# A feed-forward with held activations, a part-Strassen gate and up, and a token-major closing norm

## The chip, the core and the metric

One core of a Trainium2 chip runs the whole kernel. The metric is device microseconds of that core; the kernel before was run three times, 1559.81 to 1561.2 us, with a median of 1560.31 us.

## The reference

The function is one decoder layer over 256 tokens and a model width of 2048, in float32: a mixer (causal pooling beside a gated delta rule), an attention into 256 memory tokens, a gated feed-forward, and a last RMS norm. Only the end of it changes:

```python
def conv_glu_ffn(h, w_gate, w_up, conv_w, conv_b, w_down):
    gate = causal_dwconv(h @ w_gate, conv_w, conv_b)      # three taps over tokens, per channel
    return (jax.nn.silu(gate) * (h @ w_up)) @ w_down
...
    x = x + conv_glu_ffn(rms_norm(x, ffn_norm_g[l]), w_gate[l], w_up[l], ffn_conv_w[l], ffn_conv_b[l], w_down[l])
return rms_norm(x, final_norm_g)
```

`w_gate` and `w_up` are 2048 x 5632, `w_down` is 5632 x 2048.

## The kernel before

Every float32 operand is split into two float32r parts: `split` (L96) writes the rounded part with a cast on ACT (L97) and the remainder with a subtraction on DVE (L98). A product needs three passes: high by high, high by low, low by high.

All stages but one hold the weights. `gemm` (L144) makes 128 output channels by 256 tokens; for each of 16 k tiles a 128x128 tile of the high weights is loaded into the array and streams 512 columns (the high and the low part of the activations side by side, L139), then the low weights stream the 256 columns of the high part (L140). The two halves of the PSUM row are added afterwards (`evac`, L152). Weights come 1 MB at a time over SP's queue into three `raw` buffers, and four `whi` and four `wlo` buffers hold the split parts. The one exception is the memory's values (L690 to L692): there the activations are held, 128 tokens at a time, and 512 weight columns are streamed, three passes for each k tile and token half.

The feed-forward runs 44 times over gate tile, convolution and silu, up tile (L825 to L842). The token scale of the norm, `r3b`, is multiplied in by POOL (L831, L838), the convolution is one ACT and two DVE instructions, POOL multiplies gate by up (L841), and the result is split and kept in SBUF. Then 16 output tiles of w_down each add 44 k tiles (L854 to L858). The residual stream `xres` is channel-major, so the sum of squares of the last norm crosses partitions: a matmul with ones, a reciprocal root, a second matmul that spreads it, and 16 multiplications with nine output transfers (L861 to L875).

The order on each engine is fixed when the program is built: a scheduler takes instructions by program order as their inputs and buffers come free. Each engine then works through its list in order. Small work beside the products is put into lanes (`job`, L60) and advanced a step at a time after a matmul (`pump`, L71). Three 32 KB `big` buffers per partition hold the stages' large operands in turn.

Of the kernel before, what the change touches and what calls it, by code (L numbers as in the profile page):

```python
# [13 lines left out]
ALU = mybir.AluOpType  # L14
# [27 lines left out]
def hybrid_trunk(ctx, tc, a, out):  # L42
# [4 lines left out]
    psg = ctx.enter_context(tc.tile_pool(name="psg", bufs=3, space=bass.MemoryType.PSUM))  # L47
    psd = ctx.enter_context(tc.tile_pool(name="psd", bufs=4, space=bass.MemoryType.PSUM))
    pss = ctx.enter_context(tc.tile_pool(name="pss", bufs=1, space=bass.MemoryType.PSUM))
# [115 lines left out]
    def rfinish(sums, r, rb, name):  # L165
# [9 lines left out]
        pb = pss.tile([P, 512], F32, name=name + "pb", tag="s")  # L175
# [7 lines left out]
    def rnorm(sqs, name, bcast=True):  # L183
        r, rb = rtiles(name, bcast)

        def run():
            yield
            ps = pss.tile([P, 512], F32, name=name + "ps", tag="s")
# [5 lines left out]
    with tc.tile_pool(name="dn", bufs=1, reuse_waits="tile") as dn:  # L194
# [1 line left out]
        nc.sync.dma_start(prm, a["prm"])  # L196
        hT = big("hT", [P, KT, 2, T], F32R)
        xraw = [per.tile([P, 8, T], F32, name="xraw", tag="raw", bufs=3) for _ in range(2)]
        w0 = per.tile([P, KT, P], F32, name="w0", tag="raw", bufs=3)
# [31 lines left out]
        for c in range(4):  # L231
# [153 lines left out]
        # inverses of the 16 x 16 diagonal blocks, one block to a partition; then doubled on the tensor engine  # L385
# [320 lines left out]
    def residual(ps, f, g, ht, sqa, sql, name):  # L706
        dve.tensor_tensor(xres[:, f, :], ps[:, :T], xres[:, f, :], ALU.add)
        dve.tensor_tensor(xres[:, f, :], ps[:, T:], xres[:, f, :], ALU.add)
        if ht is not None:
            split_scaled(ht[:, f, 0, :], ht[:, f, 1, :], xres[:, f, :], pv(g, f))  # L710
        if f == 15 and sql is not None:
            act.activation(sql, xres[:, f, :], AF.Square)
            return
# [12 lines left out]
    for f in range(16):  # L726
        ps = gemm([unit(a["w_mix"][f], "wm")], lambda k: yT[:, k], [KT], "mix")
        residual(ps, f, "xa_g", h2T, sq2[0], None, "mix")
# [4 lines left out]
    oT = big("oT", [P, KT, 2, T], F32R)  # L733
    with tc.tile_pool(name="xa", bufs=1, reuse_waits="tile") as xa:
# [63 lines left out]
        h3T = big("h3T", [P, KT, 2, T], F32R)  # L798
# [9 lines left out]
        for f in range(3):  # L808
            u, ps = head[f]
            gemm_part(ps, lambda k: u(k + 12), osrc, 12, 4, KT)  # L810
            residual(ps, f, "ffn_g", h3T, sq3[0], None, "xo")
    for f in range(3, 16):
        ps = gemm([unit(a["w_xo"][f], "wo")], osrc, [KT], "xo")
        residual(ps, f, "ffn_g", h3T, sq3[0], None, "xo")
    r3, r3b, r3run = rnorm(sq3, "r3")
    job("r", r3run)

# [129 lines left out]
```

## Time and profile before

| what | value |
|---|---|
| median of three runs | 1560.31 us |
| span of the profiled execution | 1558.2 us |
| PE busy / DVE / ACT / POOL | 98% / 64% / 51% / 21% of the span |
| gate and up | 797.3 to 1296.0 us |
| down | 1296.0 to 1545.3 us |
| closing norm and output | 1545.3 to 1558.2 us |
| DMA over the span | 177 GB/s read, issued from SP alone |

The profiled execution's own time is its span, from the first to the last instruction; it lies 2.1 us under the median of the runs. Matmuls are pipelined: one has a duration of 0.40 us in the trace while the next starts 0.23 us after it, so their cost is read from start to start and not from the busy column.

### The profile page before, as it was taken

What the parts mean: (1) busy time and instruction counts of PE and PEld (TensorE: products, weight loads), DVE (VectorE), ACT (ScalarE), POOL (GpSimd) and SP (SyncE); (2) the same over time, 40 slices, a digit from 0 to 9 for tenths busy, and PEclk for the clock granted to TensorE, in tenths of its full rate; (3) what the DMA queues carried; (4) which work ended last, traced back from release to release, by engine and by line L of the source; (5) the groups of instructions that cost most, each with busy time, mean ns of one, the idle gap of its engine ahead of it and who ended that gap; (6) DMA issues with size and microseconds to landing.
All of it is one profiled execution on the core that took longest, in us unless ns stands there. A gap on an engine that the chain in (4) does not pass through costs nothing.

```text
span 1558.2 us, 22142 instructions
## 1 busy us (share of the span) xinstructions
PE 1521.3 (98%) x8714; PEld 1317.2 (85%) x8714; DVE 1002.8 (64%) x1401; ACT 798.2 (51%) x1271; POOL 330.8 (21%) x385
## 2 busy tenths in 40 slices
PE   5999999999999999999999999999999999999997
PEld 3788889888888888888888888888888888888885
DVE  7978887676544776666766666666666665545453
ACT  4555656554444554655555555555555554444442
POOL 4342532441000110000122222222222220000010
PEclk9999999999999999999999999999999999999999
DMA  5445443456555555344555555555555555555552
GB/s 202 169 164 186 148 169 122 152 186 237 191 192 193 189 183 187 136 153 154 184 186 189 181 187 183 183 188 188 190 189 189 186 183 179 185 187 188 184 192 86
DMA packets 45496, 277.31 MB, mean 178 GB/s; under 512 B 8912, under 2 KB 9552, under 8 KB 14288
## 3 DMA queue, kind: packets, MB, share of 16 engines
q1 hardware_dynamic: 45392, 275.90, 50.2%
q8 instruction: 68, 1.11, 0.3%
q14 instruction: 36, 0.29, 0.1%
HBM read 272.60 MB, written 3.28 MB: 177 GB/s over the span
## 4 chain that ended last, share of the span: by engine, by line
PE 87%; DVE 7%; issue 2%; ACT 1%; POOL 1%; DMA 1%; SPq 0%; POOLq 0%; DVEq 0%; ACTq 0%
PE up L139 10%; PE gate L139 10%; PE down L139 10%; PE up L140 5%; PE gate L140 5%; PE down L140 5%; PE mix L139 4%; PE xo L139 4%; PE xq L139 4%; PE kk L139 4%; DVE wil L98 2%; PE pvs L690 2%; PE pvs L692 2%; PE pvs L691 2%; PE xo L140 2%
## 5 line engine op out<-in xcount | busy, mean ns | idle before, releaser
L139 PE MATMUL up<-h3T,wuh 128*128 128x512 f32 x660 | 235.1, 399 | 0.0
L139 PE MATMUL gate<-h3T,wgh 128*128 128x512 f32 x660 | 235.1, 399 | 0.0
L98 DVE TENSOR_TENSOR wdl<-wd,wdh 128x1024 fp32r<-128x1024 f32 x96 | 109.4, 1140 | 124.7 <-ACT wdh L97 124.6
L140 PE MATMUL up<-h3T,wul 128*128 128x256 f32 x660 | 185.4, 281 | 0.0
L140 PE MATMUL gate<-h3T,wgl 128*128 128x256 f32 x660 | 185.3, 281 | 0.0
L97 ACT CAST wdh<-wd 128x1024 fp32r<-128x1024 f32 x96 | 93.9, 978 | 135.2 <-PE down L139 127.1
L139 PEld LDWEIGHTS up<-h3T,wuh 128*128 128x128 f32 x660 | 124.0, 188 | 28.6
L139 PEld LDWEIGHTS gate<-h3T,wgh 128*128 128x128 f32 x660 | 124.0, 188 | 28.5
L98 DVE TENSOR_TENSOR wgl<-wg,wgh 128x1024 fp32r<-128x1024 f32 x88 | 114.1, 1297 | 50.2 <-ACT wgh L97 50.2
L98 DVE TENSOR_TENSOR wul<-wu,wuh 128x1024 fp32r<-128x1024 f32 x88 | 117.0, 1330 | 26.7 <-ACT wuh L97 23.3
L140 PEld LDWEIGHTS gate<-h3T,wgl 128*128 128x128 f32 x660 | 124.7, 189 | 2.1
L140 PEld LDWEIGHTS up<-h3T,wul 128*128 128x128 f32 x660 | 124.7, 189 | 2.1
L98 DVE TENSOR_TENSOR wil<-wi,wih 128x1024 fp32r<-128x1024 f32 x78 | 100.3, 1291 | 12.1 <-ACT wih L97 11.9
L97 ACT CAST wgh<-wg 128x1024 fp32r<-128x1024 f32 x88 | 92.5, 1052 | 26.1 <-PE gate L139 22.3
L97 ACT CAST wuh<-wu 128x1024 fp32r<-128x1024 f32 x88 | 92.6, 1052 | 17.7 <-PE up L139 14.9
L139 PE MATMUL down<-aB,wdh 128*128 128x512 f32 x256 | 91.2, 399 | 0.0
L139 PE MATMUL down<-aA,wdh 128*128 128x512 f32 x256 | 91.1, 398 | 0.0
L139 PE MATMUL xq<-h2T,wqh 128*128 128x512 f32 x240 | 86.0, 399 | 0.0
L139 PE MATMUL xo<-oT,woh 128*128 128x512 f32 x240 | 85.6, 399 | 0.0
L139 PE MATMUL kk<-mT,wkh 128*128 128x512 f32 x240 | 85.6, 399 | 0.0
L139 PE MATMUL mix<-yT,wmh 128*128 128x512 f32 x240 | 85.4, 399 | 0.0
L97 ACT CAST wih<-wi 128x1024 fp32r<-128x1024 f32 x78 | 81.3, 1048 | 8.0 <-DMA wi<-in_w_in 3.2
(463 smaller groups left out, 3889.3 us busy)
## 6 DMA issues: line engine op xcount, KB each, us to landing
wg<-in_w_gate SPq DMA_DIRECT2D x44, 1024.0 KB, 4.8
wu<-in_w_up SPq DMA_DIRECT2D x44, 1024.0 KB, 4.8
wi<-in_w_in SPq DMA_DIRECT2D x39, 1024.0 KB, 4.9
wd<-in_w_down SPq DMA_DIRECT2D x32, 1024.0 KB, 5.0
wk<-in_w_k SPq DMA_DIRECT2D x16, 1024.0 KB, 4.9
wv<-in_w_v SPq DMA_DIRECT2D x16, 1024.0 KB, 4.8
wm<-in_w_mix SPq DMA_DIRECT2D x16, 1024.0 KB, 4.8
wq<-in_w_xq SPq DMA_DIRECT2D x16, 1024.0 KB, 4.8
```

The costliest lines, as they stand in the source:

```text
L97: act.copy(hi, src)
L98: return dve.tensor_tensor(lo, src, hi.bitcast(F32), ALU.subtract)
L139: pe.matmul(ps, h, full, start=kk == 0, stop=False)
L140: i = pe.matmul(ps[:, T:], l, xt[:, 0, :], start=False, stop=False)
L690: pe.matmul(pvs[m_], mT[:, kt, 0, s], h, start=kt == 0, stop=False)
L691: pe.matmul(pvs[m_], mT[:, kt, 0, s], l, start=False, stop=False)
L692: i = pe.matmul(pvs[m_], mT[:, kt, 1, s], h, start=False, stop=kt == KT - 1)
```

## The change

The gate and up weights are laid out anew as `w_gu`: for each of 11 blocks of 512 channels and each of four groups `j` of four k tiles, four pieces of 2 k tiles by 512 columns (0: gate, first two k tiles; 1: up, first two; 2: up, last two; 3: gate, last two). The activations are held in the array and 512 weight columns are streamed. `product` is one piece against 128 tokens: 2 k tiles by three passes, six matmuls of 512 columns.

In groups 0 and 1 the two token halves, the two pairs of k tiles and the pair gate and up are treated as a 2 x 2 by 2 x 2 matrix product with seven products in place of eight (Strassen's scheme in Winograd's form): four sums of activations are made once, in `stationary`; four sums of weights (`t1`, `t2`, `t3`, and `t2` plus piece 3) are made in every block. Groups 2 and 3 take eight plain products. `parts` splits a piece or a sum, its cast on ACT and its subtraction on the engine that is named: POOL or DVE. The results come token-major: six PSUM banks for the products, then DVE combines them and multiplies by the token's scale; `convolve` turns them back to channel-major with transposes on PE, makes convolution, silu and product, and stores the float32 result to DRAM (`aspill`), but for the last three blocks.

Down holds activations too, loaded back from DRAM and split again (`both`), and streams 512 columns of w_down for each step of one k tile and one half of the output. The residual stream is transposed once (`rows_of_x`) and stored, and the closing norm is taken token-major: the sum of squares then lies along a row, and the output leaves in three pieces for each token half. The raw and split buffers of the stages before move into a pool `st` that is closed, with the PSUM pools, before the feed-forward.

```diff
+    pre = ExitStack()
+    psg = pre.enter_context(tc.tile_pool(name="psg", bufs=3, space=bass.MemoryType.PSUM))
...
+    st = pre.enter_context(tc.tile_pool(name="st", bufs=1, side="right"))
+    small = [pss, "s", 1]
...
+    def stationary(f):
+        j = f // 4
+        if f == 0:
+            hps.append(big("hP", [P, 2, KT, T], F32R))
+            hps.append(big("hS", [P, 2, 4, 4, 2 * P], F32R))
+        hP, hS = hps
+        if f % 4 == 0:
+            hc[0] = hq.tile([P, 4, T], F32, name="hc", tag="hc", bufs=2)
+        h = hc[0]
+        act.activation(h[:, f % 4, :], xres[:, f, :], AF.Copy, scale=pv("ffn_g", f))
+        if f % 4 != 3:
+            return
+        split(hP[:, 0, 4 * j:4 * j + 4], hP[:, 1, 4 * j:4 * j + 4], h)
+        a11, a12, a21, a22 = (h[:, k:k + 2, t * P:(t + 1) * P] for t in range(2) for k in (0, 2))
+        ss = hq.tile([P, 4, 2, P], F32, name="ss", tag="ss", bufs=1)
+        s5, s6, s7, s3 = (ss[:, w] for w in range(4))
+        pool.tensor_tensor(s5, a21, a22, ALU.subtract)
+        dve.tensor_tensor(s7, a11, a21, ALU.subtract)
+        pool.tensor_tensor(s6, a11, s5, ALU.subtract)
+        dve.tensor_tensor(s3, a12, s6, ALU.subtract)
+        fl4 = ss.rearrange("p w k t -> p w (k t)")
+        split(hS[:, 0, j], hS[:, 1, j], fl4)
...
-        residual(ps, f, "ffn_g", h3T, sq3[0], None, "xo")
+        residual(ps, f, sq3[0], "xo")
+        stationary(f)
...
+    NB = NFF // 4
+    hP, hS = hps
+    pre.close()
+    pm = ctx.enter_context(tc.tile_pool(name="pm", bufs=1, space=bass.MemoryType.PSUM, reuse_waits="tile"))
+    small[:] = [pm, "t", 2]
+    ring = big("ring", [P, 8, 1024], F32)
+    xspill = scr.tile([2, P, D], F32, name="xspill")
+    aspill = scr.tile([NB, P, 4, T], F32, name="aspill")
+    bank = lambda name: pm.tile([P, 512], F32, name=name, tag="m", bufs=6)
+    turn = lambda name: pm.tile([P, 2, T], F32, name=name, tag="t", bufs=2)
...
+    def plain(t, k):
+        return lambda j, i: (hP[:, 0, 4 * j + k + i, half(t)], hP[:, 1, 4 * j + k + i, half(t)])
+
+    def mixed(w):
+        return lambda j, i: (hS[:, 0, j, w, half(i)], hS[:, 1, j, w, half(i)])
+
+    A11, A12, A21, A22 = (plain(t, k) for t in range(2) for k in (0, 2))
+    S5, S6, S7, S3 = (mixed(w) for w in range(4))
+
+    def product(ps, stat, j, w, first=False, last=False):
+        for i in range(2):
+            xh, xl = stat(j, i)
+            wh, wl = w[0][:, i], w[1][:, i]
+            pe.matmul(ps, xh, wh, start=first and i == 0, stop=False, skip_group_check=True)
+            pe.matmul(ps, xh, wl, start=False, stop=False, skip_group_check=True)
+            m = pe.matmul(ps, xl, wh, start=False, stop=last and i == 1, skip_group_check=True)
+        pump(m)
...
+    def rows_of_x():
+        for q in range(8):
+            t, n = q % 2, q // 2
+            yield
+            tp = pm.tile([P, 512], F32, name="xtp", tag="t", bufs=2)
+            for i in range(4):
+                pe.transpose(tp[:, half(i)], xres[:, 4 * n + i, half(t)], cv("ident"))
+            xt = fp.tile([P, 512], F32, name="xt", tag="sg", bufs=2)
+            act.copy(xt, tp)
+            nc.sync.dma_start(xspill[t, :, n * 512:(n + 1) * 512], xt)
+            yield
...
+    def convolve(b, cg, cu):
+        if b == head_b:
+            ac = acts[b] = fp.tile([P, 4, 2, T], F32R, name="ac", tag="ac", bufs=1)
+        else:
+            af = acts[b] = fp.tile([P, 4, T], F32, name="af", tag="af", bufs=2)
+        for p in range(2):
+            yield
+            gt, ut = turn("gt"), turn("ut")
+            for ps, src in ((gt, cg), (ut, cu)):
+                for i in range(2):
+                    for t in range(2):
+                        pe.transpose(ps[:, i, half(t)], src[t][:, half(2 * p + i)], cv("ident"))
+            yield
+            sg = fp.tile([P, 2, T], F32, name="sg", tag="sg", bufs=2)
+            for i in range(2):
+                f = 4 * b + 2 * p + i
+                act.activation(sg[:, i], gt[:, i], AF.Identity, bias=pv("ffn_cb", f), scale=pv("ffn_cw", 3 * f + 2))
+                for s in (1, 2):
+                    dve.scalar_tensor_tensor(sg[:, i, s:], gt[:, i, :T - s], pv("ffn_cw", 3 * f + 2 - s), sg[:, i, s:],
+                                             ALU.mult, ALU.add)
+                yield
+            act.activation(sg, sg, AF.Silu)
+            yield
...
+                dve.tensor_tensor(af[:, s], ut, sg, ALU.mult)
+            yield
+        if b < head_b:
+            nc.sync.dma_start(aspill[b], af)
...
+    raw = lambda b, j, w: fp.tile([P, 2, 512], F32, name="wr", tag="wr", bufs=6)
+
+    def load(b, j, w):
+        r = raw(b, j, w)
+        nc.sync.dma_start(r, a["w_gu"][b, j, :, w])
+        return r
+
+    def parts(src, eng):
+        h = fp.tile([P, 2, 512], F32R, name="wh", tag="wh", bufs=5)
+        l = fp.tile([P, 2, 512], F32R, name="wl", tag="wl", bufs=5)
+        act.copy(h, src)
+        eng.tensor_tensor(l, src, h.bitcast(F32), ALU.subtract)
+        return h, l
...
+    JS, JP = (0, 1), (2, 3)
+    for b in range(NB):
+        b1, b3, b5, b6, b7 = (bank(n) for n in ("b1", "b3", "b5", "b6", "b7"))
+        t2s, b21s = {}, {}
+        for j in JS:
+            f_, l_ = j == JS[0], j == JS[-1]
+            b11, b22, b12 = load(b, j, 0), load(b, j, 2), load(b, j, 1)
+            product(b1, A11, j, parts(b11, pool), first=f_)
+            product(b3, S3, j, parts(b22, dve), first=f_)
+            t1 = sumtile(1)
+            pool.tensor_tensor(t1, b11, b12, ALU.add)
+            product(b5, S5, j, parts(t1, dve), first=f_, last=l_)
+            t2 = sumtile(0)
+            dve.tensor_tensor(t2, t1, b22, ALU.add)
+            product(b6, S6, j, parts(t2, dve), first=f_, last=l_)
+            t3 = sumtile(2)
+            pool.tensor_tensor(t3, b12, b22, ALU.add)
+            product(b7, S7, j, parts(t3, dve), first=f_)
+            t2s[j] = t2
+            b21s[j] = load(b, j, 3)
+        cc = [fp.tile([P, 512], F32, name=n, tag=n, bufs=1) for n in ("c11", "c12", "c21", "c22")]
+        c11, c12, c21, c22 = cc
+        q1 = fp.tile([P, 512], F32, name="q1", tag="q1", bufs=1)
+        u2 = fp.tile([P, 512], F32, name="u2", tag="u2", bufs=1)
+        act.copy(q1, b1)
+        dve.tensor_tensor(u2, b6, q1, ALU.subtract)
+        dve.tensor_tensor(q1, b5, u2, ALU.add)
+        dve.tensor_tensor(c22, q1, b7, ALU.subtract)
+        b2 = bank("b2")
+        for j in JP:
+            f_, l_ = j == JP[0], j == JP[-1]
+            w = parts(load(b, j, 1), pool)
+            product(b3, A11, j, w)
+            product(b2, A21, j, w, first=f_)
+            w = parts(load(b, j, 2), dve)
+            product(b3, A12, j, w, last=l_)
+            product(b2, A22, j, w, last=l_)
+            w = parts(load(b, j, 0), pool)
+            product(b1, A11, j, w)
+            product(b7, A21, j, w)
+            w = parts(load(b, j, 3), dve)
+            product(b1, A12, j, w)
+            product(b7, A22, j, w)
+        dve.tensor_scalar(c22, c22, r3[:, 1:2], None, ALU.mult)
+        dve.tensor_scalar(q1, q1, r3[:, 0:1], None, ALU.mult)
+        dve.tensor_scalar(u2, u2, r3[:, 1:2], None, ALU.mult)
+        dve.scalar_tensor_tensor(c12, b3, r3[:, 0:1], q1, ALU.mult, ALU.add)
+        dve.scalar_tensor_tensor(c22, b2, r3[:, 1:2], c22, ALU.mult, ALU.add)
+        for j in JS:
+            l_ = j == JS[-1]
+            product(b1, A12, j, parts(b21s[j], pool), last=l_)
+            pool.tensor_tensor(t2s[j], t2s[j], b21s[j], ALU.add)
+            product(b7, A22, j, parts(t2s[j], dve), last=l_)
+        act.activation(c11, b1, AF.Copy, scale=r3[:, 0:1])
+        dve.scalar_tensor_tensor(c21, b7, r3[:, 1:2], u2, ALU.mult, ALU.subtract)
+        job("cv", convolve(b, (c11, c21), (c12, c22)))
...
+    arow = big("arow", [P, head_b, 4, T], F32)
+    for b in range(head_b):
+        nc.sync.dma_start(arow[:, b], aspill[b])
+        acts[b] = arow[:, b]
+    aring = big("aring", [P, 4, 4, 2, T], F32R)
+    fin = big("fin", [P, 3, D], F32)
+    for t in range(2):
+        nc.sync.dma_start(fin[:, t], xspill[t])
+    nc.sync.dma_start(fin[:, 2], a["fin_row"])
...
+    def both(n):
+        b = blocks[n]
+        s = aring[:, n % 4]
+        split(s[:, :, 0], s[:, :, 1], acts[b])
+        acts[b] = s
...
+    def down(k, t, n, w, first, last):
+        ah, al = (acts[k // 4][:, k % 4, s, half(t)] for s in range(2))
+        wh, wl = (x[:, n % 2] for x in w)
+        pe.matmul(acc[t, n], ah, wh, start=first, stop=False)
+        pe.matmul(acc[t, n], ah, wl, start=False, stop=False)
+        return pe.matmul(acc[t, n], al, wh, start=False, stop=last)
+
+    def rows(k, c):
+        rw = fp.tile([P, 2, 512], F32, name="wd", tag="wr", bufs=6)
+        nc.sync.dma_start(rw, a["w_down"][k, :, c])
+        return parts(rw, dve)
+
+    both(1)
+    steps = [(k, c) for c in range(2) for k in order[:4]] + [(k, c) for k in order[4:-2] for c in range(2)]
+    for m, (k, c) in enumerate(steps):
+        if m == 4:
+            drain("cv")
+            accs(2)
+            accs(3)
+        n = blocks.index(k // 4)
+        if k % 4 == 2 and c == 0 and 0 < n < NB - 1:
+            both(n + 1)
+        w = rows(k, c)
+        for t in range(2):
+            for n in (2 * c, 2 * c + 1):
+                i = down(k, t, n, w, k == order[0], False)
+    late = [(k, [rows(k, c) for c in range(2)]) for k in order[-2:]]
...
+        for n in range(4):
+            for k, w in late:
+                down(k, t, n, w[n // 2], False, k == order[-1])
+            c = slice(n * 512, (n + 1) * 512)
+            dve.tensor_tensor(fin[:, t, c], acc[t, n], fin[:, t, c], ALU.add)
+            junk = fp.tile([P, 512], F32, name="fj", tag="sg", bufs=2)
+            act.activation(junk, fin[:, t, c], AF.Square, accum_out=ssq[:, t, n:n + 1])
+            if n < 3:
+                pool.tensor_tensor(fin[:, t, c], fin[:, t, c], fin[:, 2, c], ALU.mult)
+        dve.tensor_reduce(msf[:, t:t + 1], ssq[:, t], AX.X, ALU.add)
+        dve.tensor_scalar(msf[:, t:t + 1], msf[:, t:t + 1], 1.0 / D, EPS, ALU.mult, ALU.add)
+        pool.tensor_tensor(rf[:, t:t + 1], msf[:, t:t + 1], cv("half")[:, :1], ALU.pow)
+        c = slice(3 * 512, D)
+        dve.scalar_tensor_tensor(fin[:, t, c], fin[:, t, c], rf[:, t:t + 1], fin[:, 2, c], ALU.mult, ALU.mult)
+        nc.sync.dma_start(out[t, :, c], fin[:, t, c])
+        c = slice(0, 512)
+        act.activation(fin[:, t, c], fin[:, t, c], AF.Copy, scale=rf[:, t:t + 1])
+        nc.scalar.dma_start(out[t, :, c], fin[:, t, c])
+        c = slice(512, 1536)
+        dve.tensor_scalar(fin[:, t, c], fin[:, t, c], rf[:, t:t + 1], None, ALU.mult)
+        nc.sync.dma_start(out[t, :, c], fin[:, t, c])
```

## Rows read from the trace of the kernel before

**Rows 1.** The page, part 1: busy time, share of the span, instructions.

```profile
PE 1521.3 (98%) x8714; PEld 1317.2 (85%) x8714; DVE 1002.8 (64%) x1401; ACT 798.2 (51%) x1271; POOL 330.8 (21%) x385
```

**Rows 2.** Stretch table: us, busy per engine (instructions), clock, DMA share, GB/s.

```profile
797.20:1296.00 498.80, 498.42 (x2823) 432.15 (x2822) 323.69 (x400) 272.53 (x398) 131.19 (x175) 1.00 0.52 185
```

**Rows 3.** Instructions of tiles: duration ns min/median/max, first and last start us.

```profile
L139 PE MATMUL gate<-h3T,wgh x660: 392/398/476, 797.3 to 1289.9; 128*128 128x512 f32 x165
...
L137 PE MATMUL down<-aC,wdh x16: 392/394/397, 1311.5 to 1544.9; 128*128 128x512 f32 x16
```

**Rows 4.** Timeline of the end: start us, us, engine, line, operation [idle before].

```profile
1549.59 5.38 DVE L874 TENSOR_TENSOR xres<-xres,rfb 128x256 f32<-128x256 f32 x16 [0.79 <-PE rfb L871]
1550.04 5.29 SPq L875 DMA_DIRECT2D out_dram<-xres  x9
```

**Rows 5.** Tile of the held-activation product: first and last of its three lines.

```profile
L690 PE MATMUL pvs<-wvh,mT x128: 389/389/396, 413.8 to 500.2; 128*128 128x512 f32 x128
...
L692 PE MATMUL pvs<-wvh,mT x128: 389/389/389, 414.3 to 500.6; 128*128 128x512 f32 x128
```

**Rows 6.** Timeline of PE where four transposes come between two k tiles.

```profile
624.89 0.39 PE L139 MATMUL xq<-h2T,wqh 128*128 128x512 f32 x1
625.12 0.74 PE L770 MATMUL tps<-cst,e 128*128 128x128 f32 x4
...
625.83 0.40 PE L139 MATMUL xq<-h2T,wqh 128*128 128x512 f32 x1
```

**Rows 7.** Timeline of POOL and of DVE over the first 35 us.

```profile
8.99 4.11 POOL L241 TENSOR_TENSOR xsq<-xraw 128x1024 f32<-128x1024 f32 x2
...
17.59 5.01 POOL L242 TENSOR_TENSOR xss<-xss,xsq 128x1024 f32<-128x1024 f32 x2
...
7.20 15.68 DVE L102 SCALAR_TENSOR_TENSOR hT<-xraw,prm,hT 128x256 fp32r<-128x256 f32 x7
...
23.94 3.24 DVE L102 SCALAR_TENSOR_TENSOR hT<-xraw,prm,hT 128x256 fp32r<-128x256 f32 x8
...
32.90 2.36 DVE L98 TENSOR_TENSOR wil<-wi,wih 128x1024 fp32r<-128x1024 f32 x2 [0.55 <-ACT wih L97]
```

**Rows 8.** Timeline of POOL and DVE in the gate stage.

```profile
918.63 0.74 POOL L831 TENSOR_TENSOR xg<-gm,r3rb 128x256 f32<-128x256 f32 x1 [4.85 <-DVE gm L156]
...
921.90 1.37 POOL L838 TENSOR_TENSOR sg<-sg,r3rb 128x256 f32<-128x256 f32 x1 [0.31 <-ACT sg L837]
...
921.45 1.23 DVE L98 TENSOR_TENSOR wul<-wu,wuh 128x1024 fp32r<-128x1024 f32 x1
```

**Rows 9.** Timeline where a DVE instruction that reads PSUM meets POOL.

```profile
347.27 1.65 POOL L679 TENSOR_TENSOR KV<-km,rmrb 128x256 f32<-128x256 f32 x1 [3.61 <-DVE km L156]
348.24 0.87 DVE L562 SCALAR_TENSOR_TENSOR yt<-otp,prm,z 128x256 f32<-128x256 f32 x2
```

**Rows 10.** Groups by line: count, busy us, mean ns, idle before.

```profile
L97 ACT CAST wuh<-wu 128x1024 fp32r<-128x1024 f32 x88 | 92.6, 1052 | 17.7 <-PE up L139 14.9 <-PE xo L137 1.9 <-ACT xos L718 0.9
...
L696 ACT ACTIVATE KV<-pvs,rmr 128x512 f32<-128x512 f32 x8 | 5.5, 690 | 3.9 <-PE pvs L692 3.9
...
L762 DVE TENSOR_SCALAR e<-e,rsum 128x256 f32<-128x256 f32 x8 | 2.5, 351 | 0.1
...
L480 DVE TENSOR_TENSOR Dm<-raw_kq,Dm 128x512 f32<-128x512 f32 x4 | 2.7, 680 | 0.0
```

**Rows 11.** Transfers: count, KB each, median us from issue to landing.

```profile
wg<-in_w_gate SPq DMA_DIRECT2D x44, 1024.0 KB, 4.8
...
us<-U SPq DMA_DIRECT2D x2, 512.0 KB, 2.6
```

**Rows 12.** PE at the program's start: a stretch as in rows 2, then the timeline.

```profile
7.10:22.70 15.60, 5.48 (x14) 0.87 (x13) 15.60 (x8) 7.94 (x18) 15.44 (x9) 1.00 0.42 165
...
25.09 0.63 PE L228 MATMUL in_k<-hT,w0h 128*128 128x512 f32 x1
...
25.73 0.63 PE L228 MATMUL in_k<-hT,w0h 128*128 128x512 f32 x1
```

More of the change, by code (lines that the diff above doesn't have):

```diff
@@ L104, in load_raw @@
     def load_raw(src, shape, name):
-        r = per.tile(shape, F32, name=name, tag="raw", bufs=3)
+        r = st.tile(shape, F32, name=name, tag="raw", bufs=3)
         nc.sync.dma_start(r, src)
@@ L197, in hybrid_trunk @@
         hT = big("hT", [P, KT, 2, T], F32R)
-        xraw = [per.tile([P, 8, T], F32, name="xraw", tag="raw", bufs=3) for _ in range(2)]
-        w0 = per.tile([P, KT, P], F32, name="w0", tag="raw", bufs=3)
+        xraw = [st.tile([P, 8, T], F32, name="xraw", tag="raw", bufs=3) for _ in range(2)]
+        w0 = st.tile([P, KT, P], F32, name="w0", tag="raw", bufs=3)
         ba = dn.tile([P, KT, 16], F32, name="ba", tag="sq", bufs=1)
@@ L810, in hybrid_trunk @@
             gemm_part(ps, lambda k: u(k + 12), osrc, 12, 4, KT)
[L811 removed]
+            residual(ps, f, sq3[0], "xo")
+    hq = pre.enter_context(tc.tile_pool(name="hq", bufs=1, reuse_waits="tile"))
+    for f in range(3):
+        stationary(f)
     for f in range(3, 16):
         ps = gemm([unit(a["w_xo"][f], "wo")], osrc, [KT], "xo")
[L814 to L815 removed]
+        residual(ps, f, sq3[0], "xo")
+        stationary(f)
@@ L844, in hybrid_trunk @@
-    sqf = ssum("sqf", 2)
-    msb = xp_.tile([P, 2], F32, name="msb")
-    def early():
-        for _ in range(3):
-            yield
-        ps = pss.tile([P, 512], F32, name="eps", tag="s")
-        colsum(ps, sqf[:1])
-        dve.tensor_scalar(msb, ps[:, :2], 1.0 / D, EPS, ALU.mult, ALU.add)
-    for f in range(16):
-        wd = a["w_down"][f]
-        ps = gemm([unit(wd[:, s:e], "wd") for s, e in ((0, 16), (16, 32), (32, 44))], asl, [16, 16, 12], "down")
-        residual(ps, f, None, None, *sqf, "down")
-        act.activation(xres[:, f, :], xres[:, f, :], AF.Copy, scale=pv("fin_g", f))
-        if f == 14:
-            job("r", early())
@@ new lines, in hybrid_trunk @@
+    accs(0)
+    accs(1)
+    blocks = [head_b, head_b + 1, *range(head_b), NB - 1]
+    order = [b * 4 + i for b in blocks for i in range(4)]
+    def both(n):
[9 more added lines that the diff above has]
+        return pe.matmul(acc[t, n], al, wh, start=False, stop=last)
@@ L871, in hybrid_trunk @@
-    pe.matmul(rfb, cv("ones"), dg, start=True, stop=True)
-    for lo, hi in ((0, 1), (1, 2), (2, 4), (4, 6), (6, 8), (8, 10), (10, 12), (12, 14), (14, 16)):
-        for f in range(lo, hi):
-            dve.tensor_tensor(xres[:, f, :], xres[:, f, :], rfb, ALU.mult)
-        nc.sync.dma_start(out[:, lo:hi, :], xres[:, lo:hi, :])
+        for n in range(4):
[7 more added lines that the diff above has]
+                pool.tensor_tensor(fin[:, t, c], fin[:, t, c], fin[:, 2, c], ALU.mult)
```

103 lines of the change are left out of this document (49 added, 54 removed).

## The prediction

> **What bounds the kernel now.** I read the page's busy times first, then the stretches of the feed-forward, then single instructions. PE is busy 98% of the span, and the reader should see in the other engines' shares that none is near it [rows 1]. In gate and up PE is busy 498.4 of 498.8 us at full clock, with DVE at 324 and POOL at 131 [rows 2]. So PE alone sets this stage, and every microsecond taken from its stream comes off the end as long as the next engine stays below it. The feed-forward starts at 797.3 us, down's last matmul starts at 1544.9 and ends 0.4 later [rows 3], the span ends at 1558.2: gate and up take 498.7 us, down 249.3, the closing norm 12.9, in all 760.9. A k tile pays 498.7 / (88 x 16) = 0.354 us for its 768 columns.
>
> **PE's new stream.** The held-activation shape is in the trace already: the values of the memory ran 384 matmuls of 512 columns from 413.8 to 500.6 us [rows 5], 86.8 / 383 = 0.2266 us each. That is less for each column than 0.354 for 768. A `product` is six of them, 1.36 us. A block has 10 products in groups 0 and 1, 16 in groups 2 and 3, and 4 late ones: 30 products, 40.8 us. New are 16 transposes a block. Four of them stretched one k tile from 0.354 to 625.83 - 624.89 = 0.94 us [rows 6], so four cost 0.59 and sixteen 2.4. PE wants 43.2 us a block, 475 in eleven, and 8 x 0.59 = 4.7 once for the transposes of x: 480 against 498.7 now. Down is 88 steps of 12 matmuls, 1056 x 0.2266 = 239.3 against 249.3.
>
> The Trainium skill (TensorE: Matmul & The Clock Gate, Back-to-back issue gap) gives about 131 ns a matmul as the sustained pace at 512 columns. By that figure down would be 138 us and the end 101 us earlier. The 384 matmuls of this trace contradict it with 0.2266, and the measurement decides.
>
> **What feeds PE.** This part decides. Each of 22 pieces and sums a block needs a cast of 1024 elements on ACT, 1.05 us [rows 10]: 23 us, and some 4 for evictions, convolution and silu, of 43. ACT is no bound. The subtractions and the sums of weights are two-input instructions with both inputs in SBUF, 30 a block. Counted from the diff: POOL has 6 in groups 0 and 1 (`b11`, `t1`, `t3`, twice), 4 in groups 2 and 3, 4 in the late part (`b21`, and `t2` plus it), 14 in all. DVE has 10, 4 and 2, 16 in all.
>
> Such instructions of POOL and DVE don't run side by side in this trace. Seven 256-element instructions of DVE took 15.68 us while POOL ran 1024-element ones back to back; the next eight, with POOL out of the way, took 3.24, or 0.40 each [rows 7]. POOL pays as well: 256 elements take it 0.74 us alone and 1.37 when they meet a 1.23 us subtraction [rows 8]. So I add them. One POOL instruction of 1024 elements with one small DVE one is 5.01 / 2 = 2.50, less 0.40 gives 2.1 for POOL. Two subtractions of DVE in a row take 2.36 with the last at its full 1.22 (a pace of 1.14) [rows 7]. A block: 14 x 2.1 = 29.4, 16 x 1.14 = 18.2, and 3 scalings of 512 elements at about 0.35 (that of 256 elements [rows 10]), 1.0. Sum 48.6 us, over PE's 43.2.
>
> DVE's other new work, 6 combinations of 512 elements (0.68 each [rows 10]), 8 taps and 2 products a block, reads one input from PSUM. Two such instructions took 0.87 together right beside a POOL instruction, no longer than without one [rows 9], so I cost their 9 us at nothing: POOL's time hides them. The Trainium skill (SBUF — State Buffer, Who interferes with whom) has this as a rule that speaks against the change: a DVE instruction with two SBUF inputs and a GpSimd one that reads SBUF exclude each other for a whole instruction, one with a single SBUF input doesn't contend. The trace agrees on both halves; were the second half wrong, a block would take 58 us and the kernel 1689.
>
> **From floor to block time.** 48.6 us, 535 in eleven blocks, holds if POOL and DVE are never both without such work. The other end has groups 0 and 1 wholly fed-bound (6 x 2.1 + 10 x 1.14 = 24.0 against 13.6 of PE) and the other 20 products with the transposes wholly PE-bound (27.2 + 2.4 = 29.6): 53.6, 590 in eleven. Five split buffers let POOL and DVE run some five pieces ahead in the second part, so I take 50, nearer the floor: 550 us.
>
> **The start.** The first two groups' activations and sums are made 30 us before they are needed, so PE could go on at once: 0 us. But the new pool's first buffers lie where the last sums of activations are made and where the old raw and split buffers stood. If the second piece waits for the last `stationary` (two casts, two subtractions and four small ones, 5 us), its load (at most 4.8 [rows 11]), cast and subtraction, it is 12 us. I take 5. A gain is excluded, as PE has no gap there now. The casts and sums of `stationary` itself lie beside the products of xo: ACT there has about 3.5 us of work for 5.67 of PE.
>
> **Handover to down.** On SP, 4 MB of stored activations, 2 MB of x and the 1 MB norm row stand ahead of most w_down pieces. About 3 MB can't leave before the last products free their buffers: 3 x 4.8 = 14 us by [rows 11], covered by up to five pieces split ahead, 5 x 2.72 = 13.6. Nothing to 10 us; I take 2. Within down DVE and ACT have one cast and one subtraction for each 2.72 us, and POOL has none, so PE is the bound: 239.3.
>
> **The closing norm.** Now 12.9 us, 5.4 of it the 16 multiplications and then the output [rows 4]. After: the end of the matmul 0.4, an addition from PSUM 0.7, a square 0.9 with its sum, three small ones and the power on POOL 1.5, one 512-element multiplication 0.8, a scaling of 1024 elements 1.1, a 512 KB transfer 2.6 [rows 11], and some queueing behind token half 0, 1 to 2: 8 to 12, I take 10. POOL's multiplication by the norm row is not on this chain but for its last one.
>
> **Sum.** 5 + 550 + 2 + 239.3 + 10 = 806.3 against 760.9: +45.4. Against the profiled execution's 1558.2 that is 1603.6; the runs' median lies 2.1 above its span, so **1606 us**. With every low end it is 1558.2 + 2.1 + (0 + 535 + 0 + 239.3 + 8 - 760.9) = 1582, with every high end (12 + 590 + 10 + 239.3 + 12) 1663; the likeliest case's own range is 1582 to 1640.
>
> **Rivals.**
> - *PE stays the bound: faster.* If POOL's 1024-element instruction or its wait costs less than the start of the program shows, a block falls to PE's 43.2. Then 5 + 475 + 5 + 2 + 239.3 + 10 = 736, -25, 1536 us. The point from which it decides: 760.9 - 5 - 2 - 239.3 - 10 = 504.6, or 45.9 us a block; for that POOL's instruction would have to be 1.9 us, not 2.1. For it: its first such instructions, squares of one tile, took 4.11 / 2 = 2.06 with DVE's in it [rows 7]. Against: the subtractions read two tiles, as the instructions of 2.50 do. 0.18, with 0.04 of it for a time within 0.2% of before (about what a measurement of this kernel can tell from no change).
> - *The clock falls where PE waits: slower still.* At the start, PE busy 5.48 of 15.6 us [rows 12], k tiles took 0.64 us after it (25.09 to 25.73), against 0.354 at full clock: that is the 1.2 GHz level. Groups 0 and 1 have PE at 13.6 of 24 us. At half clock they want 24.6 themselves, the block about 27 + 29.6 = 57, and the kernel 1606 + 77 = 1683. Against: the waits there are short, one or two us between products. 0.07.
> - *Raw buffers: slower.* Two of six stay taken by piece 3 from groups 0 and 1 to the late products, which leaves four for pieces that are held until three sums have read them. If loads come late, the feed can't run ahead: 53.6 a block and the full start, about 1652. 0.12.
>
> **Chances.** My case 0.63, the rivals 0.18, 0.07, 0.12. Faster 0.14, within 0.2% 0.04, slower 0.82. The range of 1545 to 1655 leaves out about half of each outer case.
>
> **What would show it.** Right: gate and up at 535 to 590 us; POOL's 1024-element subtractions at 2.1 to 3.2 us mean and DVE's at 1.5 to 2.5 in place of 1.2; PE waiting for `wl` of either engine, mostly in products b5, b6, b7 and the late ones; a pitch of 0.227 between matmuls in groups 2 and 3 and in down; down near 239. Wrong: PE without gaps in the blocks and POOL's subtractions beside DVE's at 2.1 and 1.2; or gaps that a weight's DMA ends; or matmul pitches of 0.43 in the blocks.

## The result and the profile after

The changed kernel takes 1727.53 us (median of 4 runs, 1725.33 to 1729.09) against 1560.76 us, a ratio of 1.1066 with a 95% interval of 1.1051 to 1.1082. The forecast, 1606 us with a range of 1545 to 1655, had the sign and missed the size by 122 us. The profiled execution took 1725.33 us, its span 1723.6.

The page's busy times, columns as in [rows 1]:

```profile
PE 1547.9 (90%) x7722; PEld 1282.0 (74%) x7722; DVE 1193.5 (69%) x1356; ACT 836.0 (49%) x1210; POOL 641.7 (37%) x364
```

Gate and up, then down, in the stretch table (columns as in [rows 2]):

```profile
801.80:1465.40 663.60, 531.24 (x2176) 415.13 (x2177) 509.43 (x381) 300.10 (x338) 438.39 (x155) 0.90 0.48 158
1465.60:1712.90 247.30, 247.30 (x1072) 199.77 (x1071) 126.20 (x115) 105.28 (x112) 5.75 (x5) 1.00 0.57 185
```

Gate and up have grown from 498.8 to 663.6 us, and PE, which never waited there, stands still for 132 of them. No other engine is busy all the time either: DVE 77%, POOL 66%. Down is PE alone, without a gap.

Groups of the steady blocks (920 to 1410 us): busy us, mean ns, idle time before and what ended it:

```profile
L941 POOL TENSOR_TENSOR wl<-wr,wh 128x1024 fp32r<-128x1024 f32 x64 | 195.2, 3056 | 33.2 <-ACT wh L940 28.7 <-DVE sg L914 2.5 <-DVE wl L941 2.0
L941 DVE TENSOR_TENSOR wl<-ring,wh 128x1024 fp32r<-128x1024 f32 x66 | 132.2, 2012 | 0.0
L941 DVE TENSOR_TENSOR wl<-wr,wh 128x1024 fp32r<-128x1024 f32 x48 | 103.6, 2158 | 10.1 <-ACT wh L940 10.1
L966 DVE TENSOR_TENSOR ring<-ring,wr 128x1024 f32<-128x1024 f32 x16 | 54.0, 3378 | 90.1 <-POOL ring L963 90.1
L963 POOL TENSOR_TENSOR ring<-wr 128x1024 f32<-128x1024 f32 x17 | 40.3, 2372 | 80.1 <-DMA wr<-in_w_gu 80.1
...
L914 DVE SCALAR_TENSOR_TENSOR sg<-gt,prm,sg 128x254 f32<-128x254 f32 x32 | 15.2, 475 | 0.5
L1000 DVE TENSOR_SCALAR u<-u,r3r 128x512 f32<-128x512 f32 x8 | 14.6, 1819 | 0.0
```

Two things are to be seen. DVE's 1024-element subtractions take 2.0 to 2.2 us in place of 1.22, its sum 3.4, even one of its scalings of one SBUF input 1.8 (0.48 in x4_no_pool); those with an input in PSUM (L914) keep their 0.47. And there are two long idle times: DVE's `t2` sum waits for POOL's `t1`, and POOL's `t1` for a raw piece's transfer.

The waits of gate and up (total us, times, longest):

```profile
DVE ring L966 <- POOL ring L963: 116.2, 22, 6.6
PEld b L877 <- POOL wl L941: 117.3, 32, 9.8
PE b L877 <- POOL wl L941: 103.5, 28, 9.3
POOL ring L963 <- DMA wr<-in_w_gu: 87.3, 19, 5.7
```

The head of one block, POOL's timeline, then DVE's, then PE's (start, us, instruction, [idle before]):

```profile
1099.22 3.38 POOL L941 TENSOR_TENSOR wl<-wr,wh 128x1024 fp32r<-128x1024 f32 x1
1106.79 2.34 POOL L963 TENSOR_TENSOR ring<-wr 128x1024 f32<-128x1024 f32 x1 [4.20 <-DMA wr<-in_w_gu]
1109.09 2.34 POOL L969 TENSOR_TENSOR ring<-wr 128x1024 f32<-128x1024 f32 x1
1111.39 3.32 POOL L941 TENSOR_TENSOR wl<-wr,wh 128x1024 fp32r<-128x1024 f32 x1
...
1101.59 2.09 DVE L941 TENSOR_TENSOR wl<-ring,wh 128x1024 fp32r<-128x1024 f32 x1
1109.17 3.34 DVE L966 TENSOR_TENSOR ring<-ring,wr 128x1024 f32<-128x1024 f32 x1 [5.48 <-POOL ring L963]
...
1105.33 0.40 PE L876 MATMUL b<-wh,hP 128*128 128x512 f32 x1
1114.76 0.80 PE L877 MATMUL b<-wl,hP 128*128 128x512 f32 x1 [9.04 <-POOL wl L941]
```

The same stretch and the two behind it, columns as in [rows 2]:

```profile
1105.30:1114.70 9.40, 0.42 (x2) 0.00 (x0) 5.53 (x2) 1.39 (x2) 7.91 (x3) 0.65 0.22 68
1114.70:1118.50 3.80, 3.74 (x9) 2.97 (x10) 3.80 (x4) 1.04 (x1) 0.01 (x1) 0.51 0.60 188
1118.50:1126.00 7.50, 6.56 (x33) 5.11 (x32) 6.97 (x6) 4.42 (x6) 6.65 (x2) 1.00 0.12 47
```

PE needs the subtraction of the block's first piece, the POOL instruction at 1111.39. It stands in POOL's list behind `t1` and `t3` of group 1, and `t1` waits from 1102.6 to 1106.8 for `b12`, whose transfer could leave only when POOL's subtraction at 1099.22 had freed a raw buffer. DVE stands too, behind its `t2`. So three in-order queues wait in a ring while PE stands 9 us. POOL itself works for 7.9 of the 9.4 us of the stretch: PE waits mostly for POOL's list to be worked off, not for an idle POOL.

### The profile page after: what moved, and what is told of

It reads as the page before. It is cut to its first block, busy times and chain, and to the rows that moved or that the text cites. A ratio compares the mean times of both kernels' runs of the same rounds, so it can differ in the third digit from the quotient of the medians.

```text
span 1723.6 us, 20473 instructions
## 1 busy us (share of the span) xinstructions
PE 1547.9 (90%) x7722; PEld 1282.0 (74%) x7722; DVE 1193.5 (69%) x1356; ACT 836.0 (49%) x1210; POOL 641.7 (37%) x364
## 4 chain that ended last, share of the span: by engine, by line
PE 51%; POOL 18%; DVE 13%; issue 8%; DMA 8%; ACT 3%; SPq 0%; POOLq 0%; DVEq 0%; ACTq 0%
POOL wl L941 8%; DMA wr<-in_w_gu 7%; PE acc L1044 5%; PE acc L1043 5%; PE acc L1045 5%; DVE wl L941 4%; PE xq L142 3%; PE xo L142 3%; PE mix L142 3%; PE kk L142 3%; POOL ring L969 3%; POOL ring L963 2%; DVE wil L101 2%; POOL ring L1006 2%; PE pvs L695 2%
## 5 line engine op out<-in xcount | busy, mean ns | idle before, releaser
L877 PE MATMUL b<-wl,hP 128*128 128x512 f32 x484 | 201.4, 416 | 107.8 <-POOL wl L941 103.5
L941 POOL TENSOR_TENSOR wl<-wr,wh 128x1024 fp32r<-128x1024 f32 x88 | 265.1, 3017 | 59.3 <-ACT wh L940 54.7
L940 ACT CAST wh<-wr 128x1024 fp32r<-128x1024 f32 x154 | 159.2, 1047 | 244.1 <-issue 121.2
L876 PE MATMUL b<-wh,hP 128*128 128x512 f32 x484 | 194.8, 403 | 6.4 <-ACT wh L940 6.3
L878 PE MATMUL b<-wh,hP 128*128 128x512 f32 x484 | 198.2, 409 | 0.0
L941 DVE TENSOR_TENSOR wl<-wd,wh 128x1024 fp32r<-128x1024 f32 x88 | 107.4, 1224 | 107.8 <-ACT wh L940 107.6
L941 DVE TENSOR_TENSOR wl<-ring,wh 128x1024 fp32r<-128x1024 f32 x88 | 170.0, 1940 | 8.6 <-ACT wh L940 8.5
L941 DVE TENSOR_TENSOR wl<-wr,wh 128x1024 fp32r<-128x1024 f32 x66 | 139.1, 2107 | 25.0 <-ACT wh L940 24.9
L1044 PE MATMUL acc<-wl,aring 128*128 128x512 f32 x320 | 127.8, 399 | 0.0
L1043 PE MATMUL acc<-wh,aring 128*128 128x512 f32 x320 | 126.2, 394 | 0.0
L1045 PE MATMUL acc<-wh,aring 128*128 128x512 f32 x320 | 125.5, 392 | 0.0
L876 PEld LDWEIGHTS b<-wh,hP 128*128 128x128 f32 x484 | 93.3, 193 | 29.4 <-ACT wh L940 6.6
L878 PEld LDWEIGHTS b<-wh,hP 128*128 128x128 f32 x484 | 94.5, 195 | 20.5
```

Of the source, the lines that this page charges most:

```text
L876: pe.matmul(ps, xh, wh, start=first and i == 0, stop=False, skip_group_check=True)
L877: pe.matmul(ps, xh, wl, start=False, stop=False, skip_group_check=True)
L878: m = pe.matmul(ps, xl, wh, start=False, stop=last and i == 1, skip_group_check=True)
L940: act.copy(h, src)
L941: eng.tensor_tensor(l, src, h.bitcast(F32), ALU.subtract)
L1043: pe.matmul(acc[t, n], ah, wh, start=first, stop=False)
```

## Experiments

Every experiment below is one run beside the kernel before (1560.3 to 1560.7), but for the two with an interval. A block's period is taken between the first matmuls of blocks; the changed kernel's are 58.8 to 63.2, the last, up to down's first matmul, 57.2, and the mean is 60.3. Sums "a block" of what the engines do are added up from the trace's intervals over the second to the tenth block.

**x1_order.** The order of POOL's list alone: `t1` and `t3` of group 1 go behind the first piece's subtraction.

```diff
-            pool.tensor_tensor(t1, b11, b12, ALU.add)
+            if f_:
+                pool.tensor_tensor(t1, b11, b12, ALU.add)
+            else:
+                with tc.issue_after(s11.ins):
+                    pool.tensor_tensor(t1, b11, b12, ALU.add)
```

> Only POOL's order is changed: the two sums of weights of group 1 (t1, t3) are put behind the subtraction of the block's first piece. Queue theory (the 9.2 us wait of PE at the start of every block comes from that order, since those sums wait for loads that wait for raw buffers): the wait falls under 3 us, the clock drops go with it, a block takes 52 us or less instead of 60.3, and the time is about 1630 us. Port theory (POOL and DVE exclude each other, and that sets the block whatever the order): the wait only moves to other products, a block stays at 57 us or more, and the time at 1690 or more.

1693.99 us. A block is about 57.2, at the port theory's edge and far from the queue theory's 52. PE's wait after the first matmul is gone; one of up to 5.6 us has come before the third product:

```profile
DVE ring L974 <- POOL ring L968: 58.6, 11, 6.8
PEld gt L907 <- DVE c L1021: 56.8, 10, 6.0
PE gt L907 <- DVE c L1021: 53.2, 10, 5.6
```

That is the previous block's convolution: its transposes wait for a combination that DVE has queued behind the `t2` sum. The order is worth 3.1 us a block, 33 in all. In the changed kernel neither POOL nor DVE works for 6.5 us a block, in x1_order for 3.5: what this order cost is gone, and what is left is the work of the two engines (51 us a block in both) and a second standstill that the edit doesn't touch.

**x2_subs_dve.** All 22 subtractions on DVE (`parts(..., pool)` becomes `parts(..., dve)`); POOL keeps its 6 sums.

> All 22 subtractions of a block go to DVE, POOL keeps its 6 sums. Port theory: exclusive work is 24 x 1.14 + 6 x 2.1 + 1.0 = 41 us, under PE's 43.2; a block takes 44 to 47 us and the time is 1545 to 1580 us. Queue theory alone: the gain is that of the order alone, as the first piece's subtraction is no longer behind POOL's sums; about 1630 us, like x1_order.

1684.18 us, about 56 a block, far from the 44 to 47 of the port theory and from the queue theory's 1630. With 16 us of POOL work a block left, POOL mostly waits for raw pieces, and DVE, in order, for POOL:

```profile
POOL ring L963 <- DMA wr<-in_w_gu: 295.1, 20, 24.6
...
DVE ring L966 <- POOL ring L963: 56.7, 13, 5.2
```

The shared path's own time fell as the port theory has it: POOL, or DVE with its inputs in SBUF, is at work for 43.1 us a block in place of 51.3 (24 x 1.14 + 6 x 2.34 + 3 x 0.48 = 42.8). But 13.1 us a block stand beside it, 6.3 in which DVE works on an input in PSUM alone and 6.8 in which neither works. The shared path is not the whole story.

**x3_fill.** The first matmul of each block but the first is issued 36 times more, so PE is busy where it waited; the repetitions are overwritten.

```diff
+            for _ in range(fill if i == 0 else 0):
+                pe.matmul(ps, xh, wh, start=True, stop=False, skip_group_check=True)
```

> The changed kernel with the first matmul of each block but the first repeated 36 times (8.2 us at full clock) where PE waits 9.2 us anyway; the result is the same. Clock theory: PE no longer falls to the 1.2 GHz level at the start of a block, where it spends some 10 us of a block now, so a block loses about 3 us and the time about 30: 1697 us. Rival (the clock costs nothing because POOL and DVE set the pace of the first group anyway): within 5 us of 1727.

1724.24 us, 3 less, though the clock is back. The changed kernel's stretch, then this one's:

```profile
900.00:1300.00 400.00, 317.58 (x1295) 248.03 (x1294) 306.31 (x227) 174.99 (x194) 263.57 (x93) 0.90 0.46 150
```

```profile
900.00:1300.00 400.00, 363.34 (x1552) 284.68 (x1551) 317.64 (x227) 176.54 (x197) 266.17 (x94) 0.98 0.47 150
```

Granted clock 0.98 in place of 0.90, and nothing gained beyond those 3 us: what PE loses at the 1.2 GHz level it would have waited anyway. The 10 us a block of the expectation hold most of PE's wait itself: in the block shown above the matmuls run at the lower level for 3.8 us only (0.51 from 1114.7 to 1118.5).

**x4_no_pool.** All subtractions and sums on DVE (`pool.tensor_tensor` becomes `dve.tensor_tensor` in the block loop); POOL has nothing there.

> All subtractions and sums of weights go to DVE, POOL has none in the blocks. Port theory: DVE has 30 x 1.14 + 9 + 1 = 44 us of work a block against 43.2 of PE, so 46 to 49 us a block and 1560 to 1600 us in time, with DVE's subtractions at 1.22 us each. Queue theory: DVE's own order brings a like wait at the start of a block, 5 us or more, and the time is over 1620.

1604.67 us, 48.5 a block in the steady part: 30 instructions on one engine are 123 us faster than the same 30 on two. Each is back at its own time:

```profile
L941 DVE TENSOR_TENSOR wl<-wr,wh 128x1024 fp32r<-128x1024 f32 x154 | 184.3, 1219 | 24.6 <-ACT wh L940 23.5
...
L963 DVE TENSOR_TENSOR ring<-wr 128x1024 f32<-128x1024 f32 x22 | 26.9, 1222 | 7.4 <-DMA wr<-in_w_gu 7.2
```

**x5_late_piece.** The loads of piece 3 of groups 0 and 1 move to the end of the block, so that they hold no raw buffer.

```diff
-            b21s[j] = load(b, j, 3)
...
+        for j in JS:
+            b21s[j] = load(b, j, 3)
```

> Only the loads of piece 3 of groups 0 and 1 move, from the end of their group to the end of the block, so that no raw buffer is held from there to the late products. Theory Q (the wait at the head of a block comes from POOL's in-order list behind loads that lack a raw buffer): with two buffers more the loads of group 1 go out earlier, the 9.2 us wait shrinks to 2 to 5 us, a block takes 54 to 57 us and the kernel 1650 to 1690. Rival E (the exclusion of POOL and DVE alone sets 60 us a block; the wait is only where it shows): block 59 to 61, kernel 1715 to 1735. A new wait of 2 to 4 us for piece 3 at the late products is possible under both and would hide up to that much.

1709.37 us, between the two ranges, with blocks of 58.4 to 64.0 (the last, with no successor, 45.5). The wait at a block's head is gone from the third block on, as theory Q said, but 7.5 to 8.3 us have come before the last late product, more than the 2 to 4 allowed for. Inconclusive on the raw buffers' price: the wait changed its place again.

**x7_order_late.** x1_order and x5_late_piece together.

> The order of x1_order (t1 and t3 of group 1 behind the first piece's subtraction on POOL) and the late piece 3 together; the work of POOL and DVE is unchanged. If the exclusion alone is left once the waits are gone, a block takes what POOL and DVE sum to with POOL's uncontended 2.34: 14 x 2.34 + 16 x 1.22 + about 1.4 of scalings = 53.7 us, kernel 802 + 591 + 247 + 11 = about 1650 (1640 to 1665). If raw buffers play no part it stays at x1_order's 57 a block and 1694. If POOL's and DVE's instructions do overlap in part, it falls below 52 and 1630.

1705.3 us, mostly 58 to 61 a block: slower than x1_order alone. The 53.7 expected of "waits gone, exclusion left" was not reached; a wait of 7.7 us stood where x1_order has its 5.6.

**x6_no_pool_plus.** x4_no_pool with the late piece 3 and the three 512-element scalings on ACT.

```diff
-        dve.tensor_scalar(c22, c22, r3[:, 1:2], None, ALU.mult)
+        act.activation(c22, c22, AF.Copy, scale=r3[:, 1:2])
```

> x4_no_pool (no POOL instruction in the blocks, 1604.7) with piece 3 loaded late and the three scalings of 512 elements moved from DVE to ACT. DVE had some 44 us of work in a block of 48.7; it loses 3 x 0.48 = 1.4. PE's stream at a pitch of 0.2335 is 180 x 0.2335 + 2.4 = 44.4. Theory: with DVE at 42.6 PE is the bound again but for a wait or two, block 45.5 to 47.5, kernel 1565 to 1592, so the change can't reach the kernel before's 1560 by a better share of the small work alone. Rival: the raw buffers were the rest, block 44.5 to 45, kernel 1550 to 1558, faster than before. If the late loads make a new wait, 1605 or more.

1564.41 us, just under the expected 1565 to 1592. From the third block to the ninth the period is 43.8 or 44.8, 44.3 in the mean and better than 45.5 to 47.5, and PE is busy 99%, with DVE at 95%:

```profile
900.00:1300.00 400.00, 395.28 (x1760) 316.75 (x1759) 381.44 (x413) 254.12 (x298) 0.00 (x0) 1.00 0.61 206
```

The first block takes 53.9 and the start 6.6 us, which is where the rest of the gain over 45.3 goes. The run has two edits beside x4_no_pool, and none tells what each of them gave.

**x8_plain.** Held activations and 512 columns without Strassen: 32 products, 16 subtractions a block on DVE, POOL idle.

> Held activations and 512 weight columns without Strassen: 32 products a block, no sums of weights, subtractions of all 16 pieces on DVE, evictions scaled on ACT and DVE, POOL idle. It tells the held activations from the Strassen part. PE: 32 x 6 x 0.2335 + 2.4 = 47.2 us a block; DVE: 16 x 1.22 + 6 + 1 = 27. Theory: PE is the bound with no wait, block 47.2 to 48, gate and up 519 to 528, kernel 802 + 523 + 249 + 11 = 1585 (1578 to 1595): held activations alone are already slower than the 45.3 a block of the kernel before, and what Strassen can give back is 2 products, 2.8 us. Rival: the pitch without DVE and POOL beside it is the 0.2267 of the memory's values, block 45.9, kernel 1560 to 1568.

1578.57 us, gate and up 802.2 to 1318.6, 46.9 a block, close to the theory's 47.2. Held activations alone are slower than the 45.3 of the kernel before; Strassen's two products bring a block to about 44.3 where the feed keeps up. All that could be won was about 1 us a block.

**x9_less_mix.** x6_no_pool_plus without the mixed activations of groups 2 and 3, which no product reads.

```diff
         split(hP[:, 0, 4 * j:4 * j + 4], hP[:, 1, 4 * j:4 * j + 4], h)
+        if j > 1:
+            return
```

> x6_no_pool_plus (1564.4) without the mixed activations of groups 2 and 3, which no product reads. The last mix stands ahead of the feed-forward's first cast: ACT there waits 1.37 us for it and casts 0.95 us, so the start gap falls from 6.6 to about 4.2 us; the loads issued at 801.7, which wait for the memory of the mix, can go out earlier, and of block 0's 53.9 us (44 in the later ones) 0 to 5 go. Theory: 1564.4 - 2.4 - (0 to 5) = 1557 to 1562, no difference from the kernel before's 1560.3 or just below it. Rival: something else sets the start (the first pieces' loads, the memory of another buffer), then 1563 to 1565, slower than before by about 0.2%.

1562.74 us, ratio 1.0014 (1.0005 to 1.0023), 0.1% over before. The start gap is 4.3, as expected; block 0 stays at 53.5.

**x10_idle_pool.** x6_no_pool_plus with 14 subtractions a block added on POOL whose results nobody reads: the shared path measured without any queue.

```diff
+        pool.tensor_tensor(row(0, 2)[:, :512], c12, row(0, 3)[:, :512].bitcast(F32), ALU.subtract)
+        for _ in range(14):
+            pool.tensor_tensor(row(0, 2), row(0, 3).bitcast(F32), row(1, 3).bitcast(F32), ALU.subtract)
```

> x6_no_pool_plus with 14 subtractions of 1024 elements more on POOL in each block, on data that nothing else reads, started when the block's c12 is written. No engine waits for them; if they cost time, it is by what two engines share. Exclusion theory (a two-input instruction of POOL and one of DVE, all inputs in SBUF, never run together): 14 x 2.34 + 30 x 1.22 = 69.4 us a block in place of 44.5, ten blocks with it, kernel about 802 + 54 + 694 + 249 + 11 = 1810 (1770 to 1830); DVE's subtractions 1.22 rise to 2 or more, its instructions with an input in PSUM (0.48, 0.69, 0.75) stay. Queue theory (the time of the changed kernel came from waits between in-order queues, not from a shared path): 1562 to 1580. In between, 1620 to 1700, the exclusion would be partial.

1886.63 us, over the range expected of a full exclusion; 73 to 75 us a block in place of 44.3. POOL, or DVE with its inputs in SBUF, is at work for 66.1 of them, within 3% of what the two sum to alone (30 x 1.14 + 14 x 2.34 and the 512-element one). The rest is 5.4 us of DVE on an input in PSUM alone, which the 69.4 left out, and 2.6 of neither. Groups, then DVE's timeline while POOL runs:

```profile
L1015 POOL TENSOR_TENSOR hS<-hS 128x1024 fp32r<-128x1024 f32 x154 | 493.0, 3201 | 12.1
L941 DVE TENSOR_TENSOR wl<-ring,wh 128x1024 fp32r<-128x1024 f32 x88 | 208.6, 2381 | 6.2 <-ACT wh L940 6.2
L914 DVE SCALAR_TENSOR_TENSOR sg<-gt,prm,sg 128x254 f32<-128x254 f32 x44 | 20.8, 472 | 0.1
```

```profile
1015.57 3.39 DVE L941 TENSOR_TENSOR wl<-ring,wh 128x1024 fp32r<-128x1024 f32 x1
1018.88 3.35 DVE L963 TENSOR_TENSOR ring<-wr 128x1024 f32<-128x1024 f32 x1
1022.16 0.74 DVE L1010 SCALAR_TENSOR_TENSOR c<-b,r3r,u 128x512 f32<-128x512 f32 x1
```

Work that nobody waits for costs 30 us a block, 2.1 for each POOL instruction, nearly its whole 2.34. A DVE instruction with two SBUF inputs waits out one of POOL's and takes 3.35; the one with an input in PSUM passes in its usual 0.74. The Trainium skill (SBUF — State Buffer, Who interferes with whom) has it so: the ports that DVE and GpSimd share are an exclusive lock, and DVE contends for it when both its inputs lie in SBUF; this run agrees. The same section exempts an instruction of one SBUF input only outside the 2-port modes, which it lets `tensor_scalar` enter. The prediction left this condition out, and the changed kernel's scalings of one SBUF input (0.48 in x4_no_pool, means of 1.0 to 1.8 beside POOL) bear it out.

**x11_early.** x9_less_mix with groups 2 and 3 of the activations split tile by tile, which frees the memory under three raw buffers 20 us earlier.

```diff
+        if j > 1:
+            split_scaled(hP[:, 0, f], hP[:, 1, f], xres[:, f, :], pv("ffn_g", f))
+            return
```

> x9_less_mix (1562.7) with the activations of groups 2 and 3 split tile by tile (one cast and one subtraction of 256 elements after each product of xo) in place of one split of four tiles behind the last product. The memory of these four tiles is where three of the six raw weight buffers lie, and the fourth raw load of the feed-forward waited for it until 800.75; now it is free after group 1, some 20 us before. ACT has one 0.42 instead of 0.49 + 1.05 between the last residual and the first weight's cast. Theory: the start gap falls from 4.3 to about 3, the six raw pieces are there when PE starts, block 0 falls from 53.5 to 47 to 50, kernel 1562.7 - 1 - (3.5 to 6.5) = 1555 to 1558, faster than before by 0.15 to 0.35%. Rival: block 0 is long because DVE makes eight subtractions and sums for each five products in groups 0 and 1 with nothing prepared; then 1560.5 to 1562, no difference that can be measured.

1562.87 us, ratio 1.001 (1.0001 to 1.0019). All six raw pieces were there before PE started, and the gap is 3.2, yet block 0 still takes 54.5, 10.7 over a block of 43.8. The rival held in part: with nothing prepared, PE waits for DVE and ACT for some 5 us up to 815, DVE making an instruction each 1.14. Matmuls at 0.43 apart in the same stretch add 2.9, the transposes of x some 2; from 815 on PE doesn't wait:

```profile
805.25 1.22 DVE L944 TENSOR_TENSOR wl<-ring,wh 128x1024 fp32r<-128x1024 f32 x1
806.38 1.22 DVE L969 TENSOR_TENSOR ring<-ring,wr 128x1024 f32<-128x1024 f32 x1
807.52 1.22 DVE L966 TENSOR_TENSOR ring<-wr 128x1024 f32<-128x1024 f32 x1
```

No version was faster than the kernel before.

## Why the prediction missed

By its own terms, against the first gate matmul of before at 797.3: the start took 4.5 (forecast 5), gate and up 663.8 (550), the handover nothing of its own (2), down 247.3 (239.3), the closing norm 10.7 (10). The errors are -0.5 + 113.8 - 2 + 8 + 0.7 = 120.0, and 45.4 + 120.0 = 165.4, the difference of the two spans.

**Wrong: "From floor to block time".** The floor was to hold "if POOL and DVE are never both without such work", and I took 50, 1.4 over it, because split buffers "let POOL and DVE run some five pieces ahead". In the trace POOL or a DVE instruction with its inputs in SBUF is at work for 51.3 us a block, and no such work runs for 9.1, together the 60.4. The 9.1 in place of 1.4 is the step that failed.

The 9.1 have three parts. For 2.6 DVE works on an input in PSUM while POOL stands, so "POOL's time hides them" holds for most of that work only: of its 9.0 us 5.8 lie beside POOL. For 3.1, at the end and the head of a block, neither works: that is the ring at group 1's `t1`. For 3.5, some 42 to 46 us into a block, neither works either: POOL has come to the `t1` of the next block's group 0, which waits for a raw piece, and DVE stands behind it, while PE works on the pieces split ahead:

```profile
1151.35 2.40 POOL L963 TENSOR_TENSOR ring<-wr 128x1024 f32<-128x1024 f32 x1 [5.30 <-DMA wr<-in_w_gu]
```

The prediction looked for the limit in busy times and in buffer counts, and never wrote out the order in which POOL and DVE issue: `t1` waits for `b12`, `b12` for a buffer that POOL itself frees, `t2` and all of DVE behind it for `t1`, the first subtraction behind `t3`. The same sum is 51.4 + 5.9 in x1_order, which takes the 3.1 away and leaves the 3.5, and 51.2 + 7.9 in x7_order_late: edits of the order move the second term, not the first.

**Mis-sized: "What feeds PE".** The mechanism was right, as x10_idle_pool shows by itself and x4_no_pool from the other side; the floor of 48.6 measured 51.3. POOL's instruction was put at 2.1, from a pair in [rows 7] less 0.40 for DVE's part; alone it takes 2.34 (the rows at 1106.79 and 1109.09), and 14 x 0.24 is 3.4. The whole of the two together, 60.3 against 50, is 10.3 a block, 113.8 over eleven.

**Mis-sized: "PE's new stream".** The pitch of [rows 5], 0.2266, is 0.233 between neighbouring matmuls in down, 6.5 of its 8 us; the other 1.6 are the sixteen transposes of the last block, which run inside down. In the blocks it is 0.2334 where nothing waits. The transposes were put too high, at 2.4 a block from four of them in [rows 6]: eight together move the next product by 1.03 - 0.23 = 0.80, so sixteen cost 1.6:

```profile
1468.10 0.39 PE L1045 MATMUL acc<-wh,ac 128*128 128x512 f32 x1
1468.34 0.60 PE L907 MATMUL gt<-cst,c 128*128 128x128 f32 x4
1468.77 0.60 PE L907 MATMUL ut<-cst,c 128*128 128x128 f32 x4
1469.13 0.48 PE L1043 MATMUL acc<-wh,ac 128*128 128x512 f32 x1
```

Neither cost anything in the blocks of the changed kernel, but PE's own block is 180 x 0.2334 + 1.6 = 43.6, and x6_no_pool_plus, with PE busy 99%, showed 44.3 in the mean: even the fed case gained 1.0 a block, not the 2.1 of the first rival.

**The rivals.** "PE stays the bound" fell. "The clock falls" has its sign in the trace (0.90) and hardly a price: x3_fill gives 3 us back, not the 77 of the rival. "Raw buffers" named one link of the ring, at the right place (POOL's wait for the transfer is 87 us), but no run priced it apart from the queue order: x5_late_piece, which frees two, gained 18 us and made a wait of its own. That stays open. So does why the pitch differs from [rows 5] by 3%.

The parts that came out near were read as single chains: the start, the handover and the closing norm, with one row each for what is late next, and adding instructions along a chain was near enough there. The start's 4.5 is in part luck: 5 was a point picked between 0 and 12, and the load that was to be late was not; PE's 6.3 us idle there end with ACT's cast, which stood behind the casts of the last `stationary`. The blocks are three queues that wait for each other.

## What to carry to other kernels

- An idle engine is no free capacity where two share a path: 14 instructions given to POOL cost DVE 30 us a block, and taking them back to the busier engine was 123 us faster.
- A floor made of busy times needs a second look at order: write each engine's list for one period, mark what each instruction waits for, and look for a ring. Reordering one queue here took away one standstill of two (3.1 of 60 us a block) and left the work on the shared path as it was.
- Price the best case first: with the feed kept up a block gained 1.0 of 45.3 us (x6_no_pool_plus), less over all blocks than the new start and the first block cost.

## What the hardware showed that was not expected

- POOL and DVE in alternation take 3.35 us for a pair whose parts take 2.34 and 1.22 alone; a scaling of one SBUF input, 0.48 alone (x4_no_pool), took 1.0 to 1.8 in the mean beside POOL.
- After the 9 us wait PE ran at the 1.2 GHz level for 3.8 us (granted clock 0.51 from 1114.7 to 1118.5, matmuls 0.43 apart from 1115.35 on). While the feed was the bound, taking most of this away gave 3 us of 1727 (x3_fill).
